# Ten orders of the products in the weight streams of a decoder trunk, with the second pair of column blocks one unit behind the first

## The chip, the cores and the metric

The kernel runs on one core of a Trainium2 chip. The metric is the device time of one execution in microseconds (us). One launch computes everything; nothing is left to the host.

## The reference

Two residual layers over 256 tokens of width 2048, each with a token mixer and a gated feed-forward part, and a last norm:

```python
for i in range(DEPTH):                       # DEPTH = 2
    h = rms_norm(x, mix_norm_w[i])
    if i % 2 == 0:
        x = x + ssd_mixer(h, ...)            # Mamba-2, 8 groups, inner width 4096
    else:
        x = x + short_conv_mixer(h, ...)     # bg * causal_dwconv(cg * h), then @ w_out
    h = rms_norm(x, ffn_norm_w[i])
    x = x + conv_ffn(h, ...)                 # silu(g) * v of causal_dwconv(h @ w_up), then @ w_down
return rms_norm(x, final_norm_w)             # d_ff = 5632
```

All weights are float32 and are read once. Nearly all of the arithmetic is in the products of activations with weights (`w_in`, `w_out`, `w_up`, `w_down`).

## The kernel before

**Two halves of a number.** A float32 product is made of several products in the type fp32r. A weight tile is split into a high part `wh` (a cast on ScalarE, L287) and a rest `wl` (a subtraction on VectorE, L288); an activation tile `hl` holds its high part in 256 columns (one for each token) and its rest in 256 more. So a block of 128 rows by 128 columns of weights needs a **wide** product, `wh` with all 512 columns of `hl` (L334), and a **narrow** one, `wl` with the first 256 columns (L335). Where the sum needs only 256 columns of result (`one=True`), the wide product is made as two of 256 columns into the same place (L331, L332).

**Streams.** A stream multiplies the activations with 512 columns of a weight matrix. It goes through the rows in *units* of 256 rows by 512 columns (KU = 2 blocks of rows, four blocks of columns): 16 products for each unit, or 24 with `one`. Results gather in two PSUM tiles of the pool `main`: `pts[0]` for the first two blocks of columns, the first pair, and `pts[1]` for the second pair. When a stream ends, `evac` takes each pair out: on ScalarE and VectorE, with norm scales, causal convolutions and gates. The pool `main` has three buffers, so the next stream's second pair goes into the buffer that this stream's first pair leaves.

**The ring of weights.** All 881 weight splits follow one plan that is written out ahead (`plan`, 880 units; the first unit is split in two halves). A raw tile is loaded by DMA from SyncE's queue (L267, four raw buffers), cast on ScalarE and subtracted on VectorE, into one of WB = 4 pairs of buffers `wh` and `wl`. A buffer is free when TensorE's last product of its unit is done. `weight_unit` takes the next unit and calls `load_unit` for as many as the ring holds.

**What sets the order.** The program is written in the order of the loops, and a scheduler (Tile, with its timeline) moves instructions on each engine where dependencies allow; instructions under `pin` stay in the order written, and weight splits have a high priority. On the chip each engine takes its instructions in the order that results. In `before` the products of the streams, the first stream apart, are free for the scheduler to move.

**Stages.** The SSD mixer: streams for B and C (`bc_stream`), then for each of 8 groups `xs_stream` (with `one`), small products of the state-space part into the PSUM pool `aux`, and `z_stream`; `residual_stream` for the projection back, half of it in the middle. Then the feed-forward part of layer 0, the short convolution's streams, and the feed-forward part of layer 1. Its last projection (L858 to L860) has tokens as rows and weights as the moving operand; it isn't a `stream`, and all its products have 512 columns. Of the products in streams 5568 are wide and 6336 narrow (768 of them belong to `one`), and 1536 are the halves of wide ones.

Of the kernel before, what the change touches and what calls it, by code (L numbers as in the profile page):

```python
# [8 lines left out]
F32 = mybir.dt.float32  # L9
# [7 lines left out]
P = 128  # L17
T = 256
D = 2048
NKD = D // P  # L20
DI = 4096
NG = 8
# [3 lines left out]
DS = 128  # L26
# [6 lines left out]
KU = 2  # L33
COLS = 512
WB = 4
# [4 lines left out]
def trunk_kernel(ctx, tc, a, out):  # L40
    nc = tc.nc
    mm = nc.tensor.matmul
# [16 lines left out]
    n_id = [0]  # L59

    def uid(s):
        n_id[0] += 1
        return f"{s}_{n_id[0]}"
# [59 lines left out]
    base, at = {}, 0  # L123
    pieces = [[] for _ in range(nrt)]
    for name, r in rows:
        base[name] = at
        lo = 0
        while lo < r.shape[0]:
            i, off = divmod(at, P)
            n = min(P - off, r.shape[0] - lo)  # L130
# [3 lines left out]
        if name == "mix":  # L134
            n_mix, at = at, P
# [90 lines left out]
    plan = []  # L226
# [31 lines left out]
    raws, units = [], []  # L258
    taken = [0]

    def load_raw():
        i = len(raws)
        w, c0, kc = plan[i]
        raw = rawpool.tile([P, KU, COLS], F32, tag="raw", name=uid("raw"))
        for k in range(0, KU, 1 if i == 0 else KU):
            n = 1 if i == 0 else KU
            ins = nc.sync.dma_start(  # L267
                out=raw[:, k : k + n, :],
                in_=w[(kc + k) * P : (kc + k + n) * P, c0 : c0 + COLS].rearrange(
                    "(k p) n -> p k n", p=P  # L270
                ),
            )
            if i < NKD // KU + 2:
                pin(ins)
        raws.append(raw)

    def load_unit():
        i = len(units)
        if i == len(raws):
            load_raw()  # L280
        raw, raws[i] = raws[i], None
        wh = wpool.tile([P, KU, COLS], F32R, tag="wh", name=uid("wh"))
        wl = wpool.tile([P, KU, COLS], F32R, tag="wl", name=uid("wl"))
        units.append((wh, wl))

        def half(ks, put):
            put(nc.scalar.copy(wh[:, ks, :], raw[:, ks, :]))  # L287
            put(tt(  # L288
                out=wl[:, ks, :], in0=raw[:, ks, :], in1=wh[:, ks, :].bitcast(F32),
                op=ALU.subtract,  # L290
            ))

        if i == 0:
            return half
        with tc.high_priority(0 if i < NKD // KU else None):
            half(slice(0, KU), pin if i < NKD // KU + 2 else lambda ins: ins)

    def weight_unit(c0, kc, ahead=WB - 1):

        i = taken[0]  # L300
        assert plan[i][1:] == (c0, kc), (plan[i], c0, kc)
        taken[0] += 1
        while len(units) < min(i + ahead + 1, len(plan)):
            load_unit()
        got, units[i] = units[i], None
        return got

    def stream(c0, hls, kcs, evac, one=False, before=None):

        pts = [psm.tile([P, 2, 512], F32, tag="main", name=uid("main")) for _ in range(2)]
        n = len(kcs)
        put = (lambda ins: ins) if before is None else pin
        for u in range(0, n, KU):
            order = [(t, k) for t in range(4) for k in range(KU)]
            if before is not None and u == 0:
                before(0)
                order.sort(key=lambda tk: tk[1])  # L320
            wh, wl = weight_unit(c0, kcs[u], WB - 1 if before is None else 0)
            for at, (t, k) in enumerate(order):
                if before is not None and at == (0 if u else 2) and u + KU < n:
                    before(u // KU + 1)
                i = u + k
                o = pts[t // 2][:, t % 2, :]
                hl = hls[i // 2][:, i % 2, :]
                lw = slice(t * P, (t + 1) * P)
                first, last = i == 0, i == n - 1
                if one:  # L330
                    put(mm(o[:, 0:T], wh[:, k, lw], hl[:, 0:T], start=first, stop=False))  # L331
                    put(mm(o[:, 0:T], wh[:, k, lw], hl[:, T : 2 * T], start=False, stop=False))  # L332
                else:
                    put(mm(o, wh[:, k, lw], hl, start=first, stop=False))  # L334
                put(mm(o[:, 0:T], wl[:, k, lw], hl[:, 0:T], start=False, stop=last))  # L335
        if before is not None:
            before(n // KU)
        if taken[0] < len(plan):
            while len(units) < min(taken[0] + WB - 1, len(plan)):
                load_unit()  # L340
        for p in range(2):
            evac(p, pts[p])

# [7 lines left out]
    def scaled(pt, r, one=False, tag="tp", pool=None):  # L351
        if one:
            s = pair_tmp(tag, pool)
            tt(out=s, in0=pt[:, :, 0:T], in1=rep2(r), op=ALU.mult)  # L354
# [48 lines left out]
    xp, xhl = [], []  # L403
    ss = small.tile([P, 2, 4], F32, tag="ss", name="ss")
    first = {}
# [50 lines left out]
    def bc_stream(g, o, before=None):  # L456

        res = []

        def evac(p, pt):  # L460
            k0 = DI // P + o * NG + g + 2 * p
            s = scaled(pt, first["r0"], True)
            y = conv(s, W_SSD, "ssdw", NCX, k0, "ssdb", "bc", bcpool)
            act(y, y, AF.Silu)
            res.append(y)

        stream(2 * DI + o * NG * DS + g * DS, xhl, range(NKD), evac, True, before)
        return res

    load_raw()  # L470
# [241 lines left out]
    for g in range(NG):  # L712
# [5 lines left out]
        m = [ssd_decay(g, part, cb) for part in range(4)]  # L718
# [57 lines left out]
    xhl, nhl = nhl, []  # L776
# [32 lines left out]
    xhl = nhl  # L809
# [103 lines left out]
```

## Time and profile before

| | |
|---|---|
| median of 2 runs | 2563.61 us (2563.5 to 2563.72) |
| the profiled execution's own time | 2563.32 us |
| its span in the trace | 2561.5 us |
| TensorE busy (products, weight loads) | 99%, 87% |
| VectorE, ScalarE busy | 70%, 52% |
| mean granted TensorE clock | 0.998 |
| DMA | 479 MB, 187 GB/s |

The span is what the trace shows between the first and the last instruction; 1.8 us of the execution's time lie around it. Products on TensorE are pipelined: the time of one product in the profile includes its way through the array, so that products overlap, and the cost of one in a row of many is the distance from its start to the next one's.

### The profile page before, as it was taken

Reading aid. Unit: us, or ns where it says so; the run is one execution under the profiler, and the core shown is the slowest. Engines: PE = TensorE matmul, PEld = TensorE weight load, DVE = VectorE, ACT = ScalarE, POOL = GpSimd, SP = SyncE. Lnnn points to the kernel's source line nnn. Section 1 sums busy time; section 2 is a strip of 40 time slices with the busy share of each in tenths; the row PEclk is TensorE's granted clock in tenths of the full one; section 3 lists DMA queues with packets and bytes.
Section 4 is the critical chain, followed back from the end, with each engine's and each line's share of the span. In section 5 each row is a group of like instructions: output and inputs, shape, how many; then the busy total and the mean of one; then the engine's idle time right before and its main releaser. Section 6 shows DMA issues by size and latency. Waiting matters only on the chain.

```text
span 2561.5 us, 38324 instructions
## 1 busy us (share of the span) xinstructions
PE 2544.6 (99%) x15101; PEld 2235.2 (87%) x15101; DVE 1790.2 (70%) x2601; ACT 1321.5 (52%) x1630; POOL 1.1 (0%) x8
## 2 busy tenths in 40 slices
PE   9999999999999999999999999999999999999998
PEld 9999998998888888888888888888888888888886
DVE  7888876788677776557776666666677774577765
ACT  5565643566555554345554444444555553455543
POOL 0000000000000000000000000000000000000000
PEclk9999999999999999999999999999999999999999
DMA  7666655665666665666665666666566666666664
GB/s 229 175 184 193 182 176 188 189 182 172 198 183 191 190 188 181 193 188 183 193 190 181 193 186 185 185 197 189 174 183 187 189 197 190 193 186 188 189 192 145
DMA packets 255737, 478.76 MB, mean 187 GB/s; under 512 B 17668, under 2 KB 29124, under 8 KB 255428
## 3 DMA queue, kind: packets, MB, share of 16 engines
q1 hardware_dynamic: 254643, 474.13, 61.3%
q8 instruction: 118, 1.93, 0.3%
q10 hardware_dynamic: 912, 2.18, 0.2%
q14 instruction: 64, 0.52, 0.1%
HBM read 474.09 MB, written 2.16 MB: 186 GB/s over the span
## 4 chain that ended last, share of the span: by engine, by line
PE 98%; DVE 1%; ACT 1%; DMA 0%; issue 0%; SPq 0%; DVEq 0%; ACTq 0%
PE main L334 50%; PE main L335 29%; PE main L331 3%; PE main L332 3%; PE main L858 3%; PE main L859 3%; PE main L860 3%; PE aux L649 1%; DVE wl L288 0%; PE aux L657 0%; DMA bias_bc<-in_ssd_dt_bias_dram 0%; PE aux L513 0%; PE aux L630 0%; DMA raw<-in_ssd_w_in_dram 0%; ACT wh L287 0%; PE aux L187 0%
## 5 line engine op out<-in xcount | busy, mean ns | idle before, releaser
L334 PE MATMUL main<-hl,wh 128*128 128x512 f32 x5568 | 1944.9, 396 | 0.2 <-DVE hl L218 0.2
L335 PE MATMUL main<-hl,wl 128*128 128x256 f32 x6336 | 1749.2, 281 | 1.8 <-DVE wl L288 1.8
L288 DVE TENSOR_TENSOR wl<-raw,wh 128x1024 fp32r<-128x1024 f32 (+1 forms) x881 | 1072.6, 1221 | 702.2 <-ACT wh L287 701.6
L287 ACT CAST wh<-raw 128x1024 fp32r<-128x1024 f32 (+1 forms) x881 | 920.8, 1048 | 1067.7 <-PE main L334 735.2
L334 PEld LDWEIGHTS main<-hl,wh 128*128 128x128 f32 x5568 | 1034.8, 188 | 236.7 <-issue 2.0
L335 PEld LDWEIGHTS main<-hl,wl 128*128 128x128 f32 x6336 | 1196.9, 189 | 17.6 <-DVE wl L288 2.7
L331 PE MATMUL main<-hl,wh 128*128 128x256 f32 x768 | 219.5, 287 | 2.5 <-DVE tp L354 1.3
L332 PE MATMUL main<-hl,wh 128*128 128x256 f32 x768 | 218.6, 285 | 0.0
L331 PEld LDWEIGHTS main<-hl,wh 128*128 128x128 f32 x768 | 148.2, 193 | 4.0 <-issue 2.0
L332 PEld LDWEIGHTS main<-hl,wh 128*128 128x128 f32 x768 | 148.3, 193 | 1.5 <-issue 1.1
L858 PE MATMUL main<-wh,hl 128*128 128x512 f32 x352 | 137.5, 391 | 0.8 <-DVE xtok L864 0.8
L859 PE MATMUL main<-wl,hl 128*128 128x512 f32 x352 | 137.4, 390 | 0.0
L860 PE MATMUL main<-wh,hl 128*128 128x512 f32 x352 | 137.0, 389 | 0.0
L370 DVE SCALAR_TENSOR_TENSOR tp<-tp,prm,tp 128x255 f32<-128x255 f32 x208 | 90.6, 477 | 0.0
L346 ACT COPY tp<-main 128x512 f32<-128x512 f32 x128 | 74.3, 580 | 26.0 <-PE main L335 26.0
L348 DVE TENSOR_TENSOR tp<-main,tp 128x512 f32<-128x512 f32 x128 | 87.4, 683 | 0.0
L858 PEld LDWEIGHTS main<-wh,hl 128*128 128x128 f32 x352 | 66.1, 188 | 15.3 <-DVE xtok L864 1.2
L860 PEld LDWEIGHTS main<-wh,hl 128*128 128x128 f32 x352 | 66.1, 188 | 14.2
L859 PEld LDWEIGHTS main<-wl,hl 128*128 128x128 f32 x352 | 66.1, 188 | 13.6
L370 DVE SCALAR_TENSOR_TENSOR g<-tp,prm,g 128x254 f32<-128x254 f32 (+1 forms) x176 | 74.6, 477 | 0.1
L368 ACT ACTIVATE g<-tp,prm,prm 128x256 f32<-128x256 f32 x88 | 48.2, 596 | 38.0 <-DVE tp L357 38.0
L357 DVE TENSOR_TENSOR tp<-tp,rrow 128x512 f32<-128x512 f32 x96 | 66.0, 688 | 1.8
(134 smaller groups left out, 966.9 us busy)
## 6 DMA issues: line engine op xcount, KB each, us to landing
raw<-in_ffn_w_up_dram SPq DMA_DIRECT2D x352, 512.0 KB, 3.7
raw<-in_ffn_w_down_dram SPq DMA_DIRECT2D x176, 512.0 KB, 4.1
raw<-in_ssd_w_in_dram SPq DMA_DIRECT2D x159, 512.0 KB, 4.5
raw<-in_sc_w_in_dram SPq DMA_DIRECT2D x96, 512.0 KB, 4.1
raw<-in_ssd_w_out_dram SPq DMA_DIRECT2D x64, 512.0 KB, 4.2
raw<-in_sc_w_out_dram SPq DMA_DIRECT2D x32, 512.0 KB, 4.2
cbc<-cs_d SPq DMA_DIRECT2D x32, 256.0 KB, 5.1
xt<-in_x_dram SPq DMA_DIRECT2D x8, 256.0 KB, 7.4
```

Of the source, the lines that this page charges most:

```text
L287: put(nc.scalar.copy(wh[:, ks, :], raw[:, ks, :]))
L288: put(tt(out=wl[:, ks, :], in0=raw[:, ks, :], in1=wh[:, ks, :].bitcast(F32), op=ALU.subtract,))
L331: put(mm(o[:, 0:T], wh[:, k, lw], hl[:, 0:T], start=first, stop=False))
L332: put(mm(o[:, 0:T], wh[:, k, lw], hl[:, T : 2 * T], start=False, stop=False))
L334: put(mm(o, wh[:, k, lw], hl, start=first, stop=False))
L335: put(mm(o[:, 0:T], wl[:, k, lw], hl[:, 0:T], start=False, stop=last))
L346: nc.scalar.copy(pb, pt[:, :, T : 2 * T])
L348: tt(out=s, in0=pt[:, :, 0:T], in1=pb, op=ALU.add)
L370: stt(out=y[:, j, d:T], in0=s[:, j, 0 : T - d], scalar=pcol(wname, (width - 1 - d) * nk + k0 + j), in1=y[:, j, d:T], op0=ALU.mult, op1=ALU ...
L858: mm(pt[:, c, :], hi_, wh[:, k, :], start=(i == 0), stop=False)
L859: mm(pt[:, c, :], hi_, wl[:, k, :], start=False, stop=False)
L860: mm(pt[:, c, :], lo_, wh[:, k, :], start=False, stop=(i == n - 1))
```

## The change

The products of a stream get an order that is written out, and TensorE keeps it. `follow` ties each product to the one ahead of it with a dependency that the scheduler must respect and that costs no semaphore. The former `stream` is split: `first_stream` is the first one, whose order was pinned already; all others go through the new `stream`. In it

- the **second pair of column blocks runs one unit behind the first**: first pair of unit 0, first pair of unit 1, second pair of unit 0, first pair of unit 2, second pair of unit 1, and so on, so that two units are in use at once; the ring still has four buffers, and two units are prepared ahead in place of three;
- within that sequence of blocks (64, 80 or 96 of them in a stream) the wide and narrow products are **arranged** in one of ten forms. Form 1 is wide, narrow by turns; 2, 6 and 9 have the narrow product one block behind (over the whole stream, in fours, in eights); 8 turns to narrow, wide after 12 blocks; 5 has two groups of four at the front and then turns. Forms 0 and 7 are two wide, two narrow; 4 is wide, narrow, narrow, wide; 3 is four wide, four narrow. `FORMS` gives the form of each stream in a fixed list of 30, over and over; streams with `one` always have form 0, which is four halves of wide products and then two narrow ones.

The number of products and of every other instruction stays the same, and the products of a block go to the same tiles.

```diff
+    def follow(inst):
+        if last_main[0] is not None:
+            tc.add_manual_dep(
+                inst.ins, last_main[0],
+                mybir.DependencyInfo(
+                    mybir.DependencyClass.NoSync, mybir.DependencyReason.DATA
+                ),
+                reason="stream order",
+            )
+        last_main[0] = inst.ins.name
+        return inst
...
+    FORMS = (1, 5, 8, 0, 2, 3, 1, 9, 4, 7, 2, 8, 6, 5, 1, 3, 2, 0, 9, 5, 7, 8, 4, 6, 3, 8, 2, 9, 1, 0)
...
+        if form == 0:
+            return grouped(2)
+        if form == 1:
+            return grouped(1)
+        if form == 2:
+            return behind(1, n)
+        if form == 3:
+            return grouped(4)
...
+        for u in range(0, n + KU, KU):
+            for p, v in ((0, u), (1, u - KU)):
+                if 0 <= v < n:
+                    blocks += [(v, t, k) for t in (2 * p, 2 * p + 1) for k in range(KU)]
+        left = {u: 16 for u in range(0, n, KU)}
+        form = 0 if one else FORMS[turn[0] % len(FORMS)]
...
+        for at, (wide, b) in enumerate(arranged(form, len(blocks))):
+            u, t, k = blocks[b]
+            if u not in held:
+                held[u] = weight_unit(c0, kcs[u], WB - 2)
...
+            if not wide:
+                follow(mm(
+                    o[:, 0:T], wl[:, k, lw], hl[:, 0:T], start=False, stop=(at == ends[t])
+                ))
...
+            left[u] -= 1
+            if left[u] == 0:
+                load_ahead(WB - 1)
...
-                    mm(pt[:, c, :], hi_, wh[:, k, :], start=(i == 0), stop=False)
-                    mm(pt[:, c, :], hi_, wl[:, k, :], start=False, stop=False)
-                    mm(pt[:, c, :], lo_, wh[:, k, :], start=False, stop=(i == n - 1))
+                    follow(mm(pt[:, c, :], hi_, wh[:, k, :], start=(i == 0), stop=False))
+                    follow(mm(pt[:, c, :], hi_, wl[:, k, :], start=False, stop=False))
+                    follow(mm(pt[:, c, :], lo_, wh[:, k, :], start=False, stop=(i == n - 1)))
```

What stands on TensorE at the start of one stream, the third of the four that project back the first half of the SSD mixer (a stream of form 0 after the change). Its first pair is `main_1287`, its second `main_1288`, and its first three units are `wh_1271`, `wh_1274` and `wh_1277` with their `wl`. Before, from the 20th product on:

```order
L335 MATMUL main_1287_8625<-hl_1082_7346,wl_1278_8574 128x256
L334 MATMUL main_1287_8625<-hl_1082_7346,wh_1277_8573 128x512
L334 MATMUL main_1288_8626<-hl_1052_7148,wh_1271_8529 128x512
L335 MATMUL main_1288_8626<-hl_1052_7148,wl_1272_8530 128x256
L334 MATMUL main_1288_8626<-hl_1052_7148,wh_1271_8529 128x512
```

So the scheduler had itself put the first pair ahead at the start of this stream: 21 products of three units, and then the second pair of the first unit. Wide and narrow products take turns, but for one place where two wide ones meet. After the change, from the stream's first product on:

```order
L435 MATMUL main_1287_8625<-hl_1052_7148,wh_1271_8537 128x512 x2
L425 MATMUL main_1287_8625<-hl_1052_7148,wl_1272_8538 128x256 x2
L435 MATMUL main_1287_8625<-hl_1052_7148,wh_1271_8537 128x512 x2
L425 MATMUL main_1287_8625<-hl_1052_7148,wl_1272_8538 128x256 x2
L435 MATMUL main_1287_8625<-hl_1054_7158,wh_1274_8559 128x512 x2
L425 MATMUL main_1287_8625<-hl_1054_7158,wl_1275_8560 128x256 x2
L435 MATMUL main_1287_8625<-hl_1054_7158,wh_1274_8559 128x512 x2
L425 MATMUL main_1287_8625<-hl_1054_7158,wl_1275_8560 128x256 x2
L435 MATMUL main_1288_8626<-hl_1052_7148,wh_1271_8537 128x512 x2
L425 MATMUL main_1288_8626<-hl_1052_7148,wl_1272_8538 128x256 x2
```

Two wide products now follow each other, then two narrow ones, and the second pair (`main_1288`) comes after 16 products and holds the first unit until the 24th. On the whole of TensorE's program a wide product follows a wide one in 1263 places, 154 before.

The end of the same stream, after the change (the last two units are `wh_1299` and `wh_1302`):

```order
L435 MATMUL main_1287_8625<-hl_1144_7752,wh_1302_8725 128x512 x2
L425 MATMUL main_1287_8625<-hl_1144_7752,wl_1303_8726 128x256 x2
L435 MATMUL main_1288_8626<-hl_1142_7742,wh_1299_8703 128x512 x2
L425 MATMUL main_1288_8626<-hl_1142_7742,wl_1300_8704 128x256 x2
L435 MATMUL main_1288_8626<-hl_1142_7742,wh_1299_8703 128x512 x2
L425 MATMUL main_1288_8626<-hl_1142_7742,wl_1300_8704 128x256 x2
L435 MATMUL main_1288_8626<-hl_1144_7752,wh_1302_8725 128x512 x2
```

The first pair is complete 16 products before the stream's end, since the second pair still has 8 of the last unit but one and 8 of the last.

More of the change, by code (lines that the diff above doesn't have):

```diff
@@ L59, in trunk_kernel @@
     n_id = [0]
+    last_main = [None]
+    def follow(inst):
[9 more added lines that the diff above has]
+        return inst
     def uid(s):
@@ L302, in weight_unit, with first_stream @@
         taken[0] += 1
-        while len(units) < min(i + ahead + 1, len(plan)):
-            load_unit()
+        load_ahead(ahead)
         got, units[i] = units[i], None
         return got
-    def stream(c0, hls, kcs, evac, one=False, before=None):
+    def first_stream(c0, hls, kcs, evac, before):
         pts = [psm.tile([P, 2, 512], F32, tag="main", name=uid("main")) for _ in range(2)]
         n = len(kcs)
-        put = (lambda ins: ins) if before is None else pin
         for u in range(0, n, KU):
@@ L324, in stream @@
                     before(u // KU + 1)
                 i = u + k
-                o = pts[t // 2][:, t % 2, :]
+                o = pts[t // 2][:, t % 2, 0:T]
                 hl = hls[i // 2][:, i % 2, :]
                 lw = slice(t * P, (t + 1) * P)
[L329 to L340, printed above, removed]
+                pin(mm(o, wh[:, k, lw], hl[:, 0:T], start=(i == 0), stop=False))
+                pin(mm(o, wh[:, k, lw], hl[:, T : 2 * T], start=False, stop=False))
+                follow(pin(mm(o, wl[:, k, lw], hl[:, 0:T], start=False, stop=(i == n - 1))))
@@ new lines, in first_stream, with arranged, behind, grouped @@
+        before(n // KU)
+        load_ahead(WB - 1)
+        for p in range(2):
+            evac(p, pts[p])
+    FORMS = (1, 5, 8, 0, 2, 3, 1, 9, 4, 7, 2, 8, 6, 5, 1, 3, 2, 0, 9, 5, 7, 8, 4, 6, 3, 8, 2, 9, 1, 0)
+    turn = [0]
+    def arranged(form, n):
+        def behind(lag, size):
+            got = []
+            for g in range(0, n, size):
+                m = min(size, n - g)
+                for b in range(m + lag):
+                    if b < m:
+                        got.append((True, g + b))
+                    if b >= lag:
+                        got.append((False, g + b - lag))
+            return got
+        def grouped(size):
+            return [
+                (w, g + b) for g in range(0, n, size) for w in (True, False)
+                for b in range(min(size, n - g))
+            ]
+        if form == 0:
[6 more added lines that the diff above has]
+            return grouped(4)
+        if form == 4:
+            return [
+                (w, b) for b in range(n) for w in ((True, False) if b % 2 == 0 else (False, True))
+            ]
+        if form == 5:
+            return grouped(4)[:8] + grouped(1)[8:]
+        if form == 6:
+            return behind(1, 4)
+        if form == 7:
+            return [x for g in range(0, n, 2) for x in
+                    ((True, g), (True, g + 1), (False, g + 1), (False, g))]
+        if form == 8:
+            return grouped(1)[:24] + [(w, b) for b in range(12, n) for w in (False, True)]
+        return behind(1, 8)
@@ new lines, in stream @@
+    def stream(c0, hls, kcs, evac, one=False):
+        pts = [psm.tile([P, 2, 512], F32, tag="main", name=uid("main")) for _ in range(2)]
+        n = len(kcs)
+        held = {}
+        blocks = []
+        for u in range(0, n + KU, KU):
[4 more added lines that the diff above has]
+        form = 0 if one else FORMS[turn[0] % len(FORMS)]
+        turn[0] += not one
+        ends = {blocks[b][1]: at for at, (_, b) in enumerate(arranged(form, len(blocks)))}
+        for at, (wide, b) in enumerate(arranged(form, len(blocks))):
+            u, t, k = blocks[b]
+            if u not in held:
+                held[u] = weight_unit(c0, kcs[u], WB - 2)
+            wh, wl = held[u]
+            i = u + k
+            o = pts[t // 2][:, t % 2, :]
+            hl = hls[i // 2][:, i % 2, :]
+            lw = slice(t * P, (t + 1) * P)
+            if not wide:
+                follow(mm(
+                    o[:, 0:T], wl[:, k, lw], hl[:, 0:T], start=False, stop=(at == ends[t])
+                ))
+            elif one:
+                for c in (0, T):
+                    follow(mm(
+                        o[:, 0:T], wh[:, k, lw], hl[:, c : c + T],
+                        start=(i == 0 and c == 0), stop=False,
+                    ))
+            else:
+                follow(mm(o, wh[:, k, lw], hl, start=(i == 0), stop=(at == ends[t])))
+            left[u] -= 1
+            if left[u] == 0:
+                load_ahead(WB - 1)
+        load_ahead(WB - 1)
@@ L465, in evac @@
             res.append(y)
-        stream(2 * DI + o * NG * DS + g * DS, xhl, range(NKD), evac, True, before)
+        c0 = 2 * DI + o * NG * DS + g * DS
+        if before is not None:
+            first_stream(c0, xhl, range(NKD), evac, before)
+        else:
+            stream(c0, xhl, range(NKD), evac, True)
         return res
```

9 lines of the change are left out of this document (6 added, 3 removed).

## The prediction

> **What bounds the kernel now.** I read the page first: its busy times, its chain of work, and the groups of products.
>
> ```profile
> span 2561.5 us, 38324 instructions
> PE 2544.6 (99%) x15101; PEld 2235.2 (87%) x15101; DVE 1790.2 (70%) x2601; ACT 1321.5 (52%) x1630; POOL 1.1 (0%) x8
> PE 98%; DVE 1%; ACT 1%; DMA 0%; issue 0%; SPq 0%; DVEq 0%; ACTq 0%
> L334 PE MATMUL main<-hl,wh 128*128 128x512 f32 x5568 | 1944.9, 396 | 0.2 <-DVE hl L218 0.2
> L335 PE MATMUL main<-hl,wl 128*128 128x256 f32 x6336 | 1749.2, 281 | 1.8 <-DVE wl L288 1.8
> ```
>
> TensorE has the end: 98% of the chain. It hardly waits: 0.2 us ahead of all wide products, 1.8 us ahead of all narrow ones. The means of 396 and 281 ns overlap, so they are no cost. The cost is the distance from start to start, which I take from counts in stretches. The first four rows count wide products in 200 us each, in the feed-forward part, where nearly everything is wide and narrow by turns; the last counts L860 in the last projection, where only products of 512 columns run, three for each count.
>
> ```profile
> 700.00:900.00 200.00, 198.01 (x571) 105.75 (x571) 1.00 0.63 189
> 900.00:1100.00 200.00, 198.89 (x571) 105.99 (x571) 1.00 0.62 189
> 1100.00:1300.00 200.00, 198.81 (x573) 106.13 (x572) 1.00 0.63 188
> 1300.00:1500.00 200.00, 198.26 (x569) 105.54 (x567) 1.00 0.61 187
> 2100.00:2200.00 100.00, 57.07 (x147) 27.41 (x147) 1.00 0.65 193
> ```
>
> 571 + 571 + 573 + 569 = 2284 pairs (one wide, one narrow) in 800 us: **350.3 ns a pair**, at a full clock (1.00). A product of 512 columns among its like costs 100 us / 441 = 227 ns. What one of 256 columns costs among its like stands in a stream with `one`, on the timeline (start and length in us):
>
> ```profile
> 58.98 0.28 PE L331 MATMUL main<-hl,wh 128*128 128x256 f32 x1
> 59.34 0.28 PE L331 MATMUL main<-hl,wh 128*128 128x256 f32 x1
> ```
>
> Between these two starts lie three products (L331, L332, L335), 0.36 us: 120 ns each. 227 + 120 = 347 ns is then the price of a pair if order plays no part, and the pairs by turns cost 350.3. They do so in two rhythms, and the timeline shows each; the first two rows are the first and last of 12 wide products in a row, the next two of 8:
>
> ```profile
> 1000.06 0.39 PE L334 MATMUL main<-hl,wh 128*128 128x512 f32 x1
> 1003.87 0.40 PE L334 MATMUL main<-hl,wh 128*128 128x512 f32 x1
> 1084.51 0.40 PE L334 MATMUL main<-hl,wh 128*128 128x512 f32 x1
> 1086.98 0.40 PE L334 MATMUL main<-hl,wh 128*128 128x512 f32 x1
> ```
>
> 3.81 us / 11 = **346.4 ns** in the low rhythm, 2.47 us / 7 = **352.9 ns** in the high one. The mean of 350.3 says that both take about half of the time. So the whole that any order of products can win, by the rhythms seen here, is 5568 x (350.3 - 346.4) = 22 us, 0.8% of the run. A measurement of this kernel tells about 2% (51 us) from no change.
>
> **The change, part by part.**
>
> *The forms.* What is new is that equal products meet: a wide one after a wide one in 1263 places (154 before), so 1109 more, and about as many more narrow ones after narrow ones. The trace has such meetings, where the scheduler made them ("x2" is a meeting; its cost runs to the next row's start):
>
> ```profile
> 918.20 0.62 PE L334 MATMUL main<-hl,wh 128*128 128x512 f32 x2
> 918.66 0.28 PE L335 MATMUL main<-hl,wl 128*128 128x256 f32 x1
> 925.95 0.64 PE L334 MATMUL main<-hl,wh 128*128 128x512 f32 x2
> 926.43 0.28 PE L335 MATMUL main<-hl,wl 128*128 128x256 f32 x1
> 509.78 0.40 PE L335 MATMUL main<-hl,wl 128*128 128x256 f32 x2
> 510.01 0.40 PE L334 MATMUL main<-hl,wh 128*128 128x512 f32 x1
> 1091.68 0.40 PE L335 MATMUL main<-hl,wl 128*128 128x256 f32 x2
> 1091.92 0.39 PE L334 MATMUL main<-hl,wh 128*128 128x512 f32 x1
> ```
>
> Two wide products took 460 ns or 480 ns, two narrow ones 230 ns or 240 ns. A group of two and two is therefore worth 690 to 720 ns, against 2 x 350.3 = 700.6 by turns: from -10.6 to +19.4 ns, and over 1109 of them from -12 to +22 us. Neither row is nearer, so I take the middle of both, 705: +4.4 ns x 1109 = **+5 us**. The other half or more of the streams (forms 1, 2, 5, 8 and 9, 18 of the 30) still run by turns, and I leave them at 350.3.
>
> The Trainium skill ("TensorE: Matmul & The Clock Gate", section "Back-to-back issue gap") gives a warm product N / 2.4 + 2.5 ns: a pair would take about 325 ns by that estimate, and the trace's 350.3 doesn't agree. Had the grouped orders that price, its sum would be an estimated 141 us less for all pairs.
>
> *The streams with `one`.* Four halves and two narrow ones are six products of 256 columns as before, at the 120 ns of the rows above: 0.
>
> *The second pair one unit behind.* It keeps two units of weights in use, so that a buffer, once free, has two units of work until it is needed full. A unit is 8 pairs, 2.8 us, and two are 5.6 us. What fills a buffer is a cast and a subtraction behind the release. Here is the slowest refill of all stages behind the mixer, in layer 1's feed-forward part: the unit's last product, its cast, its subtraction (the first of "x2").
>
> ```profile
> 1868.49 0.40 PE L335 MATMUL main<-hl,wl 128*128 128x256 f32 x2
> 1869.81 1.99 ACT L287 CAST wh<-raw 128x1024 fp32r<-128x1024 f32 x2
> 1871.75 2.35 DVE L288 TENSOR_TENSOR wl<-raw,wh 128x1024 fp32r<-128x1024 f32 x2
> ```
>
> It is done by about 1871.75 + 1.2 = 1872.97, 4.5 us after the release: inside 5.6 us. So outside the mixer the shorter ring costs 0, and what hides it is 1.1 us of slack at worst. In the mixer VectorE is nearer its limit, and there a refill can take longer:
>
> ```profile
> 100.00:320.00 220.00, 219.41 (x1613) 201.53 (x1612) 193.98 (x403) 140.26 (x173) 0.00 (x0) 1.00 0.65 190
> 602.27 0.28 PE L335 MATMUL main<-hl,wl 128*128 128x256 f32 x1
> 603.26 1.03 ACT L287 CAST wh<-raw 128x1024 fp32r<-128x1024 f32 x1
> 608.01 2.35 DVE L288 TENSOR_TENSOR wl<-raw,wh 128x1024 fp32r<-128x1024 f32 x2
> ```
>
> VectorE is busy 193.98 of 220 us (88%), and the unit released at 602.27 is full at about 609.2, 6.9 us later, 1.3 us too late for two units of work. From 52 to 603 us there are 20 refills over 5.6 us, by 23 us together: the upper end. The lower end is 0, because these refills are late by VectorE's queue and not by the release (the cast had been done at 604.29, and the subtraction stood behind other work until 608.01). That work is there whether the buffer is freed at 602 or 605, and the buffer is needed at the same time as before. Also, the scheduler runs the first pair 21 products ahead at a stream's start already, with three units in use, and TensorE's waits for `wl` come to the 1.8 us above. I take 0, the nearer end. A wait of this kind would hold everything behind that product on TensorE, the small `aux` products of the state-space part too, and VectorE's evacuations that wait for those.
>
> *What evacuation gets.* The first pair is complete 16 products before a stream's end, and its buffer is wanted again 16 products after the next one's start; before, that was 8 and about 21. Both leave over 5 us (29 and 32 products at 175 ns), and the waits of TensorE have one single wait of a product for an evacuation:
>
> ```profile
> PE main L331 <- DVE tp L354: 1.3, 1, 1.3
> ```
>
> So I take 0, between -1.3 us (that wait gone) and +1.3 us (one more of its kind). `follow` adds no semaphore: 0. The DMAs of raw tiles and of the decay rows keep their order on SyncE's queue within three loads: 0.
>
> **Sum**, against the profiled execution: 2563.3 + 5 + 0 + 0 = **2568 us**; the median of the runs shown, 2563.6, is the same within 0.3 us.
>
> **The rivals.**
>
> 1. *The low rhythm everywhere.* If each meeting of equal products brings the rhythm back to its low form, all pairs cost 346.4: 2563.3 - 22 = 2542 us. For it: the rows at 918.20 and 509.78 are no dearer than low pairs. Against: 925.95 and 1091.68.
> 2. *The high rhythm everywhere.* Groups at their dear end, +22, and the remaining 5568 - 2 x 1109 = 3350 pairs by turns at 352.9, +9: 2594 us.
> 3. *The ring runs short in the mixer* (slower). Place: stretches like 600 to 610 us, where state-space work stands ahead of a subtraction on VectorE. Point: a refill of over 5.6 us whose lateness moves with the release. Price: up to 23 us, with the forecast's groups 2568 + 23 = 2591 us; for over 2% it needs rival 2 as well (2617).
> 4. *Grouping hides the fixed part of a product* (faster). 227 - 120 = 107 ns for 256 columns more, so 120 - 107 = 13 ns of each product go with no column. If groups hid it, a pair would cost 2 x 13 less than 347: 2563.3 - 5568 x (350.3 - 321) = 2400 us. Against it are the rows themselves: 441 equal products in 100 us pay it all the same. This is what the skill's price above would come near to.
>
> **How the numbers follow.** Forecast, 2556 to 2580: 0.58. Rival 1: 0.18. Rival 2: 0.12, rival 3: 0.10 (of which 0.03 with 2, over 2%). Rival 4: 0.01, and 0.01 for what I don't see. The range goes from 2542, rival 1, to 2594, which holds rivals 2 and 3 apart. Within 2%: 0.96; slower by more: 0.03; faster: 0.01.
>
> **What would show it.** Counts of wide products in 200 us of the feed-forward part between 566 and 577 (352.9 and 346.4 ns) say the rhythms set it; above 580, rival 4. Sums of two and two outside 690 to 720 ns would break the first term. Waits of TensorE for `wl` above some 5 us, before 650 us, would be rival 3; waits for evacuation would break the zero there. Wrong altogether I would be if four equal products in a row cost otherwise than two.

## The result and the profile after

| | before | after |
|---|---|---|
| median | 2563.61 us (2563.5 to 2563.72) | 2587.35 us (2584.23 to 2590.47) |
| profiled execution, its span | 2563.32, 2561.5 us | 2590.47, 2588.7 us |
| ratio | | 1.0094, 95% interval 1.0073 to 1.0116 |
| mean granted TensorE clock | 0.998 | 0.995 (0.997 in the run of 2584.23) |

The changed kernel is 0.9% slower: clear of the noise, within the 2% that the chances went by, and inside the range (2542 to 2594), but 19 us above the forecast of 2568 and outside the 2556 to 2580 that had the chance of 0.58. The page after:

```profile
span 2588.7 us, 38343 instructions
PE 2553.8 (99%) x15101; PEld 2242.5 (87%) x15101; DVE 1796.6 (69%) x2601; ACT 1325.8 (51%) x1628; POOL 1.1 (0%) x8
```

The same instructions on TensorE, 9 us more of busy time, 27 us more of span. First the counts of wide products in the four stretches of the feed-forward part where before had 571, 571, 573 and 569 (the wide products of the new stream are at L435):

```profile
700.00:900.00 200.00, 186.53 (x570) 97.95 (x569) 1.00 0.65 188
900.00:1100.00 200.00, 189.95 (x571) 100.94 (x569) 1.00 0.64 187
1100.00:1300.00 200.00, 189.58 (x572) 100.94 (x571) 1.00 0.64 188
1300.00:1500.00 200.00, 189.09 (x568) 101.34 (x568) 1.00 0.64 188
```

2281 pairs in 800 us, 350.7 ns each, where before took 350.3. (Such a count takes in products that only overlap an end of the stretch, so it can be one too high; that makes about 0.6 ns a pair, in both kernels alike.) The ten orders, taken together, cost nothing there. What TensorE waited for is the other view (columns: total us, times, longest us):

```profile
PE aux L733 <- ACT xs L678: 5.8, 5, 1.7
PE main L425 <- DVE wl L302: 5.3, 5, 2.2
PE aux L163 <- DVE prm L164: 3.8, 2, 2.9
PE aux L201 <- DVE dg L193: 3.1, 1, 3.1
PE main L435 <- DVE hl L232: 1.8, 1, 1.8
```

All of these are new or larger: before, TensorE waited 1.8 us for `wl` and 0.3 us in any small product (`aux`). L733 are the transposes of `xs` ahead of the state products, L163 turns the parameters, L201 spreads a norm's factor, L425 is a narrow product.

To see how this adds up I went through the starts of TensorE's products in each trace. From the distance of each product of a stream to the next start I took 120 ns (256 columns) or 226.7 ns (512 columns; together 346.7, the low rhythm). What is left over I call *rhythm* where it is under 40 ns, and a *stall* where it is 40 ns or more. The table splits both at 660 us, where the mixer's small products have ended; its last projection runs on to 738 us. The last column is the time that TensorE's clock was granted at half (0.5) between 20 and 2540 us.

| kernel | median us | ratio, 95% interval | rhythm, to 660 / behind | stalls, to 660 / behind | half clock |
|---|---|---|---|---|---|
| before | 2563.6 | | 3.7 / 17.3 | 14.7 / 1.9 | 0 |
| after | 2587.4 | 1.0094 (1.0073 to 1.0116) | 2.1 / 19.9 | 35.8 / 4.8 | 17.1 |
| no ties | 2566.2 | 1.0013 (1.0003 to 1.0023) | 3.4 / 18.7 | 14.8 / 1.9 | 0 |
| no lag | 2581.4 | 1.0074 (1.0059 to 1.0089) | 2.9 / 20.0 | 26.5 / 6.0 | 23.9 |
| all form 1 | 2589.2 | 1.0097 (1.0082 to 1.0112) | 3.6 / 18.7 | 33.1 / 4.8 | 20.5 |
| forms 3 and 1 | 2588.7 | 1.0101 (1.0086 to 1.0116) | 3.6 / 19.5 | 33.3 / 3.3 | 10.2 |
| ties behind the mixer only | 2567.0 | 1.0012 (1.0003 to 1.0022) | 3.5 / 19.3 | 15.9 / 2.2 | 3.4 |
| ties in the mixer only | 2587.8 | 1.0095 (1.0081 to 1.0108) | 2.1 / 19.2 | 35.1 / 3.6 | 17.1 |
| all form 0 | 2574.8 | 1.0042 (1.0028 to 1.0056) | 1.5 / 8.8 | 32.2 / 1.9 | 10.2 |
| xs transposes later | 2591.8 | 1.0106 (1.0093 to 1.0120) | 2.6 / 19.9 | 35.7 / 3.6 | 13.7 |
| all form 2 | 2593.9 | 1.0114 (1.0101 to 1.0128) | 2.6 / 27.3 | 31.8 / 1.9 | 10.2 |
| better, without lag | 2559.1 | 0.9983 (0.9974 to 0.9992) | 3.7 / 9.0 | 15.6 / 6.0 | 0 |
| better, with lag | 2555.1 | 0.9964 (0.9950 to 0.9978) | 3.8 / 9.1 | 15.0 / 1.9 | 0 |

The medians come from several sessions; each ratio is against the kernel before in its own session (2562.8 to 2564.9 us). The other columns are of one profiled execution each.

Before to after the span grew by 27.2 us: rhythm 21.0 to 22.0 (+1.0), stalls up to 660 us +21.1, stalls behind +2.9, and the small products' own time 66.5 to 68.7 (+2.2).

Not every stall is a wait. In three stretches of the changed kernel the granted clock (the number behind TensorE's busy time and count) is a half:

```profile
44.66:51.48 6.82, 5.54 (x26) 0.50 0.43 148
119.75:123.16 3.41, 3.41 (x12) 0.50 0.54 154
659.06:665.88 6.82, 5.41 (x17) 0.50 0.53 208
```

From start to start a wide product takes 0.42 us there and a narrow one 0.22:

```profile
119.89 0.63 PE L435 MATMUL main<-hl,wh 128*128 128x512 f32 x1
120.31 0.41 PE L425 MATMUL main<-hl,wl 128*128 128x256 f32 x1
120.53 0.63 PE L435 MATMUL main<-hl,wh 128*128 128x512 f32 x1
```

Such products make 3.6 of the 35.8 us of stalls and 2.4 of the 4.8 us behind, as the last stretch crosses the line at 660. The kernel before has no such stretch between 14 and 2553 us. So of the 27.2 us some 17.9 are waits of TensorE of over 0.15 us (6.7 us in all before, 24.6 after), 6.0 are products of streams at half clock, and 1.0 is rhythm; the 2.3 that are left are shorter gaps and small products. Each stretch begins within 1.2 us of the end of one of the three longest waits (2.9, 2.2 and 3.1 us). That the waits bring the low clock is likely, but it is not shown: with ties behind the mixer only, TensorE waits 8.3 us as it does with no ties, and yet has 3.4 us at half clock where no ties has none.

### The profile page after: what moved, and what is told of

The parts are those of the page before. It is cut to its first block, busy times and chain, and to the rows that moved or that the text cites. A ratio compares the mean times of both kernels' runs of the same rounds, so it can differ in the third digit from the quotient of the medians.

```text
span 2588.7 us, 38343 instructions
## 1 busy us (share of the span) xinstructions
PE 2553.8 (99%) x15101; PEld 2242.5 (87%) x15101; DVE 1796.6 (69%) x2601; ACT 1325.8 (51%) x1628; POOL 1.1 (0%) x8
## 4 chain that ended last, share of the span: by engine, by line
PE 75%; DVE 0%; ACT 0%; issue 0%; ACTq 0%
PE main L435 44%; PE main L425 22%; PE main L961 3%; PE main L962 3%; PE main L963 3%; PE aux L921 0%; PE aux L752 0%; PE aux L201 0%; DVE xtok L967 0%; PE aux L208 0%; ACT xtok L936 0%; DVE yg L788 0%; DVE wl L302 0%; ACT wh L301 0%; PE aux L760 0%; DVE xtok L938 0%
## 5 line engine op out<-in xcount | busy, mean ns | idle before, releaser
L435 PE MATMUL main<-hl,wh 128*128 128x512 f32 x5568 | 1856.1, 397 | 2.3 <-DVE hl L232 1.8
L425 PE MATMUL main<-hl,wl 128*128 128x256 f32 x6272 | 1502.1, 281 | 5.3 <-DVE wl L302 5.3
L301 ACT CAST wh<-raw 128x1024 fp32r<-128x1024 f32 (+1 forms) x881 | 923.2, 1048 | 1117.9 <-PE main L435 755.9
L425 PEld LDWEIGHTS main<-hl,wl 128*128 128x128 f32 x6272 | 1142.0, 189 | 96.4 <-DVE wl L302 6.8
L435 PEld LDWEIGHTS main<-hl,wh 128*128 128x128 f32 x5568 | 979.9, 189 | 165.3 <-DVE hl L232 2.0
L430 PE MATMUL main<-hl,wh 128*128 128x256 f32 x1408 | 231.5, 286 | 1.3 <-DVE tp L453 1.3
L430 PEld LDWEIGHTS main<-hl,wh 128*128 128x128 f32 x1408 | 196.9, 193 | 2.6 <-issue 2.4
L469 DVE SCALAR_TENSOR_TENSOR g<-tp,prm,g 128x255 f32<-128x255 f32 (+1 forms) x176 | 73.8, 476 | 0.1
L467 ACT ACTIVATE tp<-tp,prm,prm 128x256 f32<-128x256 f32 x88 | 48.0, 593 | 0.0
L469 DVE SCALAR_TENSOR_TENSOR xs<-tp,prm,xs 128x253 f32<-128x253 f32 (+2 forms) x96 | 40.8, 474 | 0.0
```

The lines of the kernel that those rows point to most:

```text
L425: follow(mm(o[:, 0:T], wl[:, k, lw], hl[:, 0:T], start=False, stop=(at == ends[t])))
L430: follow(mm(o[:, 0:T], wh[:, k, lw], hl[:, c : c + T], start=(i == 0 and c == 0), stop=False,))
L435: follow(mm(o, wh[:, k, lw], hl, start=(i == 0), stop=(at == ends[t])))
L467: act(y[:, j, :], s[:, j, :], AF.Identity, bias=pcol(bname, k0 + j), scale=w)
L469: stt(out=y[:, j, d:T], in0=s[:, j, 0 : T - d], scalar=pcol(wname, (width - 1 - d) * nk + k0 + j), in1=y[:, j, d:T], op0=ALU.mult, op1=ALU ...
```

## The experiments

**No ties.** The changed kernel, with `follow` leaving the products untied:

```diff
-        if last_main[0] is not None:
+        if False:
```

> The changed kernel with the same written order, but the scheduler is free again to move the streams' products (no tie from each to the next). In the changed kernel's trace the rhythm of the products costs as much as before (21.9 us above 120 ns and 227 ns a product, 21.0 before), and stalls of over 40 ns between products of the streams and what follows them cost 40.5 us (16.6 before), 38 of them before 700 us. Theory pin (the fixed order holds products behind waits that the scheduler went around): stalls fall to about 17 us, time near 2565 us. Theory lag (the second pair one unit behind, with the shorter ring, is what starves the mixer): the written order still has the lag, so stalls stay at 30 to 40 us and the time at 2580 to 2590. Theory forms (groups of equal products cost): stays at 2580 to 2590 too.

2566.2 us: 21 of the 24 us are back, with lag and forms written as before. The waits of TensorE are small again (the two rows that answer to those above):

```profile
PE main L425 <- DVE wl L302: 1.1, 1, 1.1
...
PE aux L201 <- DVE dg L193: 1.0, 1, 1.0
```

So the ties are needed for the loss. How the tied order ends in a wait shows around one of the stalls of the changed kernel. Its timeline of VectorE there (start, length, engine and line, operation, output and inputs):

```profile
216.59 1.65 DVE L469 SCALAR_TENSOR_TENSOR xs<-tp,prm,xs 128x253 f32<-128x253 f32 x4
218.17 1.21 DVE L302 TENSOR_TENSOR wl<-raw,wh 128x1024 fp32r<-128x1024 f32 x1
...
219.70 0.95 DVE L721 TENSOR_TENSOR decay<-decay,cb 128x768 f32<-128x768 f32 x1
...
220.96 1.81 DVE L721 TENSOR_TENSOR decay<-decay,cb 128x768 f32<-128x768 f32 x2
...
223.10 0.47 DVE L469 SCALAR_TENSOR_TENSOR xs<-tp,prm,xs 128x253 f32<-128x253 f32 x1
...
223.89 0.47 DVE L469 SCALAR_TENSOR_TENSOR xs<-tp,prm,xs 128x253 f32<-128x253 f32 x1
224.28 3.48 DVE L302 TENSOR_TENSOR wl<-raw,wh 128x1024 fp32r<-128x1024 f32 x3
```

ScalarE's rows there (L301 is the cast of a weight unit, L678 the SiLU of `xs`; in square brackets the idle time ahead of a row):

```profile
221.34 1.03 ACT L301 CAST wh<-raw 128x1024 fp32r<-128x1024 f32 x1
225.05 1.05 ACT L301 CAST wh<-raw 128x1024 fp32r<-128x1024 f32 x1 [2.68 <-issue]
226.00 0.63 ACT L678 ACTIVATE xs<-xs 128x512 f32<-128x512 f32 x1
```

And TensorE's, the last product ahead of the transposes and the transposes (in square brackets the wait):

```profile
224.57 0.40 PE L435 MATMUL main<-hl,wh 128*128 128x512 f32 x1
226.68 0.66 PE L733 MATMUL aux<-ident,xs 128*128 128x128 f32 x4 [1.71 <-ACT xs L678]
```

VectorE worked without a pause from 216.6 to 227.8 us, with the convolution of `xs`, the decay products and the gate's split, and left the subtractions to the end: none starts between 218.17 and 224.28, then three in a row. But the wait of 1.71 us is not VectorE's. The convolution of `xs` ends at 224.36, before TensorE's last product ahead of the stall ends (224.97). What comes late is ScalarE's SiLU (to 226.63), because a cast stands in front of it, and the cast stood until 224.98 for a buffer of the ring of weights. The timeline names no releaser there; the semaphore's record in the trace does: it is that same last product of TensorE. So TensorE waits for a SiLU that stood behind a cast that waited for TensorE. The waits of 1.0, 1.0 and 1.7 us ahead of the transposes at 279.80, 571.65 and 624.75 us have the same chain: product ended, cast, SiLU, transposes. With no ties VectorE has the subtractions spread over the same work:

```profile
218.35 0.87 DVE L232 SCALAR_TENSOR_TENSOR hl<-yg,prm,hl 128x256 fp32r<-128x256 f32 x2
219.13 2.69 DVE L721 TENSOR_TENSOR decay<-decay,cb 128x768 f32<-128x768 f32 x3
221.74 1.22 DVE L302 TENSOR_TENSOR wl<-raw,wh 128x1024 fp32r<-128x1024 f32 x1
...
224.27 1.22 DVE L302 TENSOR_TENSOR wl<-raw,wh 128x1024 fp32r<-128x1024 f32 x1
225.40 1.28 DVE L736 TENSOR_TENSOR xdt<-aux,dt 128x512 f32<-128x512 f32 x2
226.60 1.22 DVE L302 TENSOR_TENSOR wl<-raw,wh 128x1024 fp32r<-128x1024 f32 x1
```

There ScalarE's SiLU of `xs` is done at 207.13, and the transposes come at 221.37, 14 us later; in the changed kernel they start 0.05 us behind the SiLU. Where the scheduler may not move the products, it lines up the small products and the work of VectorE and ScalarE otherwise too, and on the chip this line leaves no slack.

**Where.** Two kernels with the tie switched by a flag at the end of the mixer; here the first, the other with True and False exchanged.

```diff
+    tied = [False]
...
-        if last_main[0] is not None:
+        if tied[0] and last_main[0] is not None:
...
     mixer.close()
+    tied[0] = True
```

> The changed kernel with its lag and its ten forms everywhere, but the products are tied to each other only behind the mixer; in the mixer the scheduler is free. Theory pin-in-mixer (tied products in the mixer let small products and narrow products stand where they wait): stalls before 660 us fall from 35.8 to about 15 us as in the kernel with no ties, time 2564 to 2568. Rival (the ties cost by themselves, wherever they are): about half of the 24 us stays, 2574 to 2580.

> The opposite: products are tied only up to the end of the mixer, free behind it. Theory pin-in-mixer: stalls before 660 us stay at 33 to 36 us, time 2583 to 2590. Rival (ties cost wherever they are): 2574 to 2580.

2567.0 and 2587.8 us, as the theory of the mixer had it, to the place: the whole loss is made by tied products in the mixer, where VectorE was busy 88% of the time between 100 and 320 us before. Behind the mixer ties cost nothing that these runs tell, as long as the lag is there too.

**No lag.** The changed kernel with its ties and forms, the four column blocks of a unit one behind the other, and three units prepared ahead again:

```diff
-        for u in range(0, n + KU, KU):
-            for p, v in ((0, u), (1, u - KU)):
-                if 0 <= v < n:
-                    blocks += [(v, t, k) for t in (2 * p, 2 * p + 1) for k in range(KU)]
+        for v in range(0, n, KU):
+            blocks += [(v, t, k) for t in range(4) for k in range(KU)]
...
-                held[u] = weight_unit(c0, kcs[u], WB - 2)
+                held[u] = weight_unit(c0, kcs[u], WB - 1)
```

> The changed kernel with the ties and the ten forms, but without the lag: all four column blocks of a unit follow each other, and three units are prepared ahead. Theory lag: stalls back to about 17 us, time near 2565. Theory pin: stalls stay at 30 to 40 us, time 2580 to 2590. Theory forms: stays there too. In every case the forms' rhythm stays near 20 to 24 us above the bare products.

2581.4 us, between the theories: TensorE's waits fall from 24.6 to 17.0 us, not to the 6.7 of before. The stalls up to 660 us fall from 35.8 to 26.5, of which 7.2 are products at half clock. The waits that stay are others (in this kernel L698 multiplies B by C, L423 is a narrow product, L433 a wide one):

```profile
PE aux L163 <- DVE prm L164: 3.5, 1, 3.5
PE main L433 <- DVE hl L232: 2.9, 1, 2.9
PE aux L698 <- DVE prm L164: 2.7, 1, 2.7
...
PE main L423 <- DVE wl L302: 1.1, 1, 1.1
```

The waits for `wl` (5.3 us with the lag, 1.1 us without) and of the transposes of `xs` (5.8 us with it, none without) need lag and ties together: with the lag and no ties they are 1.1 us and none. Those at the parameters near 40 and 102 us come with the ties alone. At the gate, near 650 us, TensorE waits 4.9 us with both, 3.1 with ties alone, 2.8 with the lag alone and 0.4 before. So of the 17.9 us of waits that the change adds, about 10 stand without the lag, and about 8 need it. This split rests on one trace of each kernel; by the times the lag's part is about 6 us, and the intervals of the two ratios overlap.

**Form 1 everywhere.** `FORMS = (1,)`.

> The changed kernel with ties and lag, and form 1 (wide, narrow by turns) in all streams with wide products. In the changed kernel's trace a stream of form 1 ran at 0.07 or at 6.1 to 6.7 ns a pair above 347 ns and never changed in the middle, so with nothing to change the rhythm some 4400 pairs of the feed-forward and short-convolution stages should keep one rhythm: either about 0 or about 29 us of excess there. Theory forms (groups cost the 24 us): time 2560 to 2565 in either rhythm. Theories pin and lag: stalls stay at 30 to 40 us, and the time is near 2568 in the low rhythm or near 2597 in the high one.

2589.2 us: the groups of equal products are not what costs, and the stalls stay (33.1 us). One part of the expectation failed: the rhythm did change on the way. It was a pure one for hundreds of us and then the other (counts of wide products; the last column of numbers in brackets ahead of the clock is that of the weight loads):

```profile
700.00:900.00 200.00, 199.28 (x575) 107.62 (x575) 1.00 0.66 190
1120.00:1320.00 200.00, 200.00 (x567) 106.35 (x566) 1.00 0.64 187
1550.00:1750.00 200.00, 200.00 (x578) 108.16 (x578) 1.00 0.64 190
```

578 in 200 us are 346.0 ns a pair, 567 are 352.7 (by the starts, without the products at the ends of a stretch, 346.7 and 353.3). It went high at 1004 us, low at 1490, high at 1859. At 1490 and 1859 small products stood between; at 1004 a projection's streams began, with none.

**Forms 3 and 1.** `FORMS = (3, 1, 1, 1, 1, 1, 1)`.

> The changed kernel with ties and lag; of each seven streams with wide products the first has form 3 (four wide, four narrow), the other six form 1. In the changed kernel's trace each of the five streams by turns that came right behind a stream of form 3 ran in the low rhythm (0.07 to 0.18 ns a pair above 347). If four and four resets the rhythm, excess outside the mixer falls from 16 us to about 3 us: 0.07 ns x 6/7 + 4.0 ns x 1/7 a pair; the time is 10 to 14 us below the changed kernel's if the stalls stay (2573 to 2577). If those five were chance, about half of the streams run high and nothing is gained (2580 to 2590).

2588.7 us: nothing gained, so the five streams were chance. A stream of form 3 ended at 712 us and another at 869; behind the first the rhythm was low, behind the second high (347.8 and 351.9 ns a pair):

```profile
720.00:840.00 120.00, 119.28 (x345) 64.38 (x344) 1.00 0.66 189
880.00:1000.00 120.00, 120.00 (x341) 63.89 (x340) 1.00 0.65 187
```

The second was entered in the low rhythm and left in the high one. Behind the mixer there are ten streams of form 3: behind four of them the rhythm is low, behind six high, and in at least six it changed.

**Form 0 and form 2 everywhere.** `FORMS = (0,)` and `FORMS = (2,)`.

> The changed kernel with form 0 (two wide, two narrow) in all streams with wide products, ties and lag as they are. In the changed kernel's trace the eight streams of form 0 cost 1.5 to 2.5 ns a pair above 347, whatever rhythm came before them. If that holds everywhere, the excess behind 660 us falls from 19.9 to 8 to 9 us, the mixer's stalls stay at 33 to 36, and the time is 2574 to 2578. If it held only between other forms, the excess stays near 20 and the time at 2583 to 2590.

> The changed kernel with form 2 (the narrow product one block behind the wide one over the whole stream) in all streams with wide products. Its eleven streams in the changed kernel cost 6.2 to 6.6 ns a pair outside the mixer. If it always runs in the high rhythm, the excess behind 660 us rises from 19.9 to 28 to 30 us: time 2594 to 2600. If the rhythm is a matter of what came before the stream, excess stays at 15 to 22 us and the time at 2583 to 2590.

Form 0 gave 2574.8 us, with 8.8 us of rhythm behind the mixer instead of 19.9; form 2 gave 2593.9 us, with 27.3, just under what was expected. Two stretches of 200 us, of form 0:

```profile
900.00:1100.00 200.00, 180.27 (x576) 87.18 (x574) 1.00 0.64 190
1100.00:1300.00 200.00, 180.35 (x575) 87.31 (x574) 1.00 0.65 189
```

and of form 2:

```profile
900.00:1100.00 200.00, 199.46 (x571) 106.34 (x570) 1.00 0.60 187
1100.00:1300.00 200.00, 199.31 (x569) 106.01 (x568) 1.00 0.60 187
```

So the order of products does matter, by 19 us between these two kernels and 13 us between form 0 and the changed kernel: two and two is dependably near the low rhythm (1.8 ns a pair over 346.7), a narrow product one block behind is near the high one most of the time.

**The transposes of xs later.** The changed kernel with `small_products` (the transposes and the state products) called from within the z stream, and the transposes tied there:

```diff
+            if hook is not None and at == hook_at:
+                hook()
...
-        xdt = ssd_xdt(g, xs)
-        ys = ssd_y(g, m, xdt, xs)
-        zs = z_stream(g)
+        zs = z_stream(g, small_products, 0 if g == NG // 2 else 92 if g < 2 else 76)
+        ys = got[0]
```

> The changed kernel, but the transposes of xs (and with them the state products behind them) are tied into the sequence of products at a later place: after 76 of the z stream's products (92 in the first two groups, 0 in the fifth). In the changed kernel they stood 58 to 60 products behind the last xs product in groups 2, 3, 4, 6 and 7, and waited for ScalarE's SiLU, 6.7 us in all; before they stood 67 or more behind and did not wait. Theory too-early: these waits go to about 0 and the time falls by 5 to 8 us, to 2579 to 2583. Rival (VectorE and ScalarE are late for something anyway, and the wait only moves on to the next product that needs them): stalls before 660 us stay at 33 to 36 us and the time at 2585 to 2590.

2591.8 us: my theory fell, and the rival held. The transposes no longer wait (L735 here), but the narrow products now do, at the same times (L427):

```profile
PE main L427 <- DVE wl L302: 11.2, 10, 2.2
...
PE aux L735 <- ACT xs L680: 1.2, 3, 0.6
```

At 224.44 us, for one, the narrow product behind the wide one waits 1.65 us for a subtraction. Here it is VectorE that is late: it starts this subtraction at 225.21, behind the decay products, the gate's split and the convolution, though the cast was done at 220.42. So with the transposes out of the way the next thing that the same stretch has late is `wl`, and moving one of the two only moves the wait.

**A better version.** Before's order in the mixer (by turns, no lag, no ties), form 0 with ties behind it, without and with the lag there. The edit from the kernel with ties behind the mixer only, for the second:

```diff
+        lag = KU if tied[0] else 0
...
-                held[u] = weight_unit(c0, kcs[u], WB - 2)
+                held[u] = weight_unit(c0, kcs[u], WB - 2 if tied[0] else WB - 1)
...
-        form = 0 if one else FORMS[turn[0] % len(FORMS)]
+        form = 0 if tied[0] else 1
```

> A version made from what the runs showed: in the mixer the order of the kernel before (wide, narrow by turns, no lag, no ties), behind it form 0 with ties and no lag. If the mixer's stalls are those of before (about 15 us) and form 0 costs 1.8 ns a pair in some 4540 pairs (8.2 us, where before has 17), the time is 8 to 9 us under the kernel before: 2554 (ratio 0.9966). If ties cost outside the mixer too, it is 2563 or more.

> The better version once more, with the second pair of column blocks one unit behind outside the mixer only (form 0, ties), and the order of the kernel before in the mixer. Without the lag the tied streams outside the mixer had 6.0 us of stalls, with it 1.9 to 2.2 us. If that holds, 4 us below the version without: about 2555 us (ratio 0.997). If the lag makes no difference, 2559.

Without the lag 2559.1 us: better than before, but 5 us above what was expected, since tied products without lag stall for 6.0 us behind the mixer (1.9 before). With the lag 2555.1 us, ratio 0.9964 (0.9950 to 0.9978): the same stalls as before and half of its rhythm. So behind the mixer the lag is worth having, together with ties; the stalls (6.0 against 1.9 us) show it more clearly than the two ratios, whose intervals just overlap. In the stretch from 900 to 1100 us (wide products at L437):

```profile
900.00:1100.00 200.00, 180.15 (x575) 87.17 (x575) 1.00 0.62 189
```

575 against 571 before: 347.8 ns a pair.

## Why the prediction was right or wrong

- *What bounds the kernel, and how much order can win*: right. Nothing went under 346 ns a pair or over 354 at a full clock and without stalls, in any of 13 kernels, and the fourth rival (the fixed 13 ns of a product hidden by grouping) got nothing. The Trainium skill's estimate of about 325 ns a pair that the prediction worked out ("TensorE: Matmul & The Clock Gate", section "Back-to-back issue gap") was met in no run.
- *The forms, +5 us (-12 to +22)*: measured +1.0, inside. The two parts of it were off in opposite ways. Two and two came to 2 x (346.7 + 1.8) = 697 ns, in the lower half of 690 to 720. And the forms that I left at 350.3 did not stay there: in the changed kernel the streams with the narrow product behind (2, 6, 9) cost 352.1 to 352.6, form 1 351.2, forms 5 and 8 349.5 to 349.9. The mean was right by luck more than by the step. One sign of being wrong altogether was met in the small: four equal products in a row did cost otherwise than two, 350.5 ns a pair in form 3 against 348.5 in form 0. Over the eight streams of form 3 that is 1 us.
- *The streams with `one`, 0*: right (-0.3 ns for each three products before and after).
- *The ring behind the mixer, 0*: right. With ties behind the mixer only and with lag, stalls there are 2.2 us, 1.9 before. The 4.8 of the changed kernel are 2.4 without the products at half clock.
- *`follow`, 0, and the ring in the mixer, 0*: **this is the step that failed**, by the whole loss of 24 us. I priced a tie as what it adds to TensorE's program, a semaphore or none, and left out that it takes from the scheduler the freedom to put another product in the place of one that would wait, and that this reorders VectorE and ScalarE too. My reason for the lower end ("that work is there whether the buffer is freed at 602 or 605, and the buffer is needed at the same time as before") took before's places on the queues as given, and looked at VectorE alone: in the changed kernel casts on ScalarE stood for a buffer until TensorE's last product freed it, and held up what stood behind them. The runs without ties and without lag show it: with lag and a free scheduler the stalls up to 660 us are 14.8, as before; with ties 35.8.
- *The clock*: the prediction counted every product at a full clock and had no term for a lower one. Half clock took 6.0 us in the streams of the profiled run. All kernels with ties in the mixer have 10 to 24 us at half clock, the others 0 to 3.4.
- *Rival 3* had the place (the mixer) and the sign, and its mark was met: waits for `wl` of 5.3 us, where I had written 5. Its price of 23 us came near the measured 21 of stalls partly by luck, as 3.6 of these are products at half clock. Its mechanism was half right: refills whose lateness moves with the release are in the trace, as casts that stand in front of the SiLU, but only with the ties; and about 10 of the 17.9 us of new waits need no lag at all.
- *Evacuation, 0*: right; the one wait of 1.3 us is still there. The range held because it reached to rivals 2 and 3; the forecast itself had no term for the tied order.

What stays open: why the scheduler's order with ties leaves so little slack (its own estimates are not in a trace), what sets the rhythm of a stream by turns, and what brings the clock down to a half.

## What to carry to other kernels

A tie between instructions on the engine that sets the end is not free because it costs no semaphore: ask what the scheduler did with the freedom, above all in stages where the engines that feed it are nearly full, and fix an order only where they have slack. Where a product of 256 and one of 512 columns alternate and TensorE is the bound, try two and two. When a wait is moved and comes back at the same time under another name, look for what is late on each engine at that time: here it was ScalarE's cast the first time and VectorE's subtraction the second. And look at the granted clock by stretches before calling lost time a wait: the mean of 0.995 against 0.998 held 17 us at half clock.

## What the runs showed of the hardware that I had not expected

- Products by turns run in one of two rhythms, 346.7 or 353.3 ns a pair (578 or 567 pairs in 200 us), for hundreds of us, at a full clock and without a wait. Small products in between changed it (at 1490 and 1859 us in the kernel of form 1), four equal ones in a row did in at least six of ten streams, and it also changed with nothing in between (at 1004 us).
- Two wide and two narrow products cost 348.3 ns a pair wherever they stood (1.5 to 2.5 ns over 346.7 in each of the eight streams of the changed kernel, 575 or 576 pairs in 200 us in the kernel of form 0).
- In the kernels with ties in the mixer the granted clock fell to 0.5 for 3.4, 6.8 or 10.2 us at a time. In these stretches a product of 256 columns took 213 ns from start to start and one of 512 columns 427, where it is 120 and 227 at a full clock.
